# Moving a decoder step's merge gates ahead of the attention, and the sample's paged attention into the prompt's units

## The chip, the cores and the metric

One core of a Trainium2 chip runs the whole step as one program. The metric is device time in microseconds, as a median over runs. The engines are TensorE (PE; its weight loads are PEld), VectorE (DVE), ScalarE (ACT), GpSimd (POOL) and SyncE (SP, which here only issues transfers). A framework schedules the program ahead of time: each engine gets a fixed list of instructions, in an order that a scheduler chose from the order of the source, and runs it from top to bottom.

## What is computed

One layer of a hybrid decoder, for a prompt (1 sequence of 1024 tokens) and a sample (8 sequences of 4 new tokens, each with 8192 cached ones). Cut to what matters:

```python
h = rmsnorm(x, g_norm1) * (1 + scale1) + shift1          # scale, shift, gate: silu(c) @ w_ada
za, zq, zkv, zg, zm = split(h @ w_in)                    # u|v, q, k/v of 3 branches, branch gates, merge gates
ya = chunk_spatial_gating(u, layernorm(v))
kc, vc = compress_blocks(cached and new rows)            # one row per block of 64 tokens
o_cmp = softmax(q kc) vc                                 # its probabilities also choose 16 blocks
o_sel = softmax(q k_chosen) v_chosen                     # the sample: from the paged cache
o_win = softmax(q k_window) v_window                     # last 512 tokens
yb = g0 * o_cmp + g1 * o_sel + g2 * o_win
x = x + gate1 * ((sigmoid(zm_a) * (ya @ w_a) + sigmoid(zm_b) * (yb @ w_b)) @ w_out)
x = x + gate2 * conv_ffn(rmsnorm(x, g_norm2) * (1 + scale2) + shift2)
```

Shapes: d_model 1024, 8 query heads and 2 key heads of 64, 1056 columns (1024 prompt, 32 sample). All in float32; large products are made of three float32r products of high and low parts.

## The kernel before

Activations lie with features on partitions and the 1056 columns in the free dimension. A **dense output** is one 128-feature slice of h @ w_in: 8 k-tiles by 3 products by 3 column ranges (`CH`), 72 matmuls (`dense`, `products`). There are 22 of them behind u: four queries (`query`), two keys (`key`) and sixteen merge gates (`merge_gate`). Queries, keys and gates go to DRAM and are read back later.

A **compression step** `compress(n)`, n = 0 to 15, loads 32 pages of a sample sequence (4 MB, tensor `pcmp`, two such steps a sequence) into one of two buffers and runs 64 matmuls; `compress_end(n)` finishes it. Steps 9 to 15 stand in a loop over j = 0 to 6 (lines 719 to 728), each after two dense outputs. That loop holds all queries, both keys and gates 0 to 7. Then PG and R2B, the pools of the pages, are released.

Then comes the sample's attention (from line 737): the compressed branch with the choice of blocks, which gives the mask `MB`; two **windows** (`sample_window`, four sequences each, 2 MB); and 32 **paged pieces** (`sel_unit(b, u)`, four per sequence, each 16 pages or 2 MB of `psel`). A piece is a chain: scores (PE, line 869), mask and maximum (DVE, 870 and 872), exp (ACT, 873), four transposes (PE, 877), a copy out of PSUM (ACT, 878), 16 value matmuls (PE), a copy (ACT, 891). After u = 3 the four pieces are merged (897 to 921). The first eight pieces (`EARLY`) and gates 8 to 15 stand in the source one after the other; the scheduler interleaves them. Inside the gates stand three late modulation chunks (`ada_late`: 2 MB of `w_ada`, 8 matmuls of 512 columns and 4 small ones).

Last comes the prompt's attention: 32 **units** (i, j), query tile i = 0 to 7 of 128 rows and head pair j = 0 to 3. `attend_n(n)` makes scores, maxima, exponentials and scales of unit n; `combine_n(n - 2)` transposes (line 1113), copies (1116) and multiplies with the values for the unit two back. A unit of tile i works on i + 1 key tiles in the chosen branch and up to five in the window branch, so units grow from i = 0 to i = 7. `key_tiles(j)` reads a key back and splits it into high and low parts (lines 949 to 952); `queries(i)` does so for a query tile (966, 967). The remaining 24 pieces are put behind `combine_n`, six in each eight units, and five more modulation chunks at n = 1, 4, 12, 20 and 28. Pieces, windows and chunks share page-size buffers: two in pool R3S, and two more in R3C for half of the pieces once the gates are done.

Matmuls of the unit and of the piece are issued by the helper `mm`, which is line 55 for all of them. Pages are issued on SP (three of four groups for `psel`) and on ACT (`load_pages`).

Of the kernel before, what the change touches and what calls it, by code (L numbers as in the profile page):

```python
# [49 lines left out]
def step_kernel(tc, A):  # L50
# [30 lines left out]
    def slot(dt=F32):  # L81
        return S([128, R], dt, "S", NS)
# [146 lines left out]
    def ada_chunk(ch, tiles, per, own):  # L229
        ps = pU()  # L230
        for h in range(2):
            for g in range(4):
                k = 4 * h + g
                mm(ps[32 * g:32 * g + 32], sc[:, k], tiles[k // per][:, (k % per) * 512:(k % per + 1) * 512],
                   h == 0, h == 1)
        modev = own()
        act.copy(modev, ps)
# [4 lines left out]
        dve.tensor_tensor(mod[:, ch * 4:ch * 4 + 4], v[:, :, 0:9],  # L242
                          bada[:, ch * 4:ch * 4 + 4, None].to_broadcast([128, 4, 9]), op=OP.add)

# [449 lines left out]
    R2B = new_pool("r2b", "right")  # L694
# [24 lines left out]
    for j in range(7):  # L719
        if j < 4:  # L720
            query(j)
        elif j < 6:
            key(j - 4)
        else:
            merge_gate(7, slot())
        merge_gate(j, slot())
        compress(LATE + j)
        compress_end(LATE + j)
    PG.release()
    R2B.release()  # L730
# [3 lines left out]
    for b in range(8):  # L734
        pool.dma_start(A["o_wsv"][b][508:512], vs_new[4 * b:4 * b + 4, 128:256])


    R3 = new_pool("r3")
    R3S = new_pool("r3s")
    GR = C2([128, 2, 3])  # L740
# [3 lines left out]
    for gr in range(2):  # L744
# [16 lines left out]
        nm = R3([128, 1], F32, "sm1", 12)  # L761
        dve.tensor_reduce(nm, ps[:, 0:128], axis=AX.X, op=OP.max, negate=True)
        p = R3([128, 128], F32, "ou", 5)
        su = R3([128, 1], F32, "sm1", 12)
        act.activation(p, ps[:, 0:128], AF.Exp, bias=nm, accum_out=su)
        r = R3([128, 1], F32, "sm1", 12)
# [37 lines left out]
    def sample_window(gr):  # L804
        ps = pU()
        st = R3S([128, 4, 4, 256], F32, "st", 2).rearrange("p a b c -> p (a b c)")
        wk = st[:, 0:2048].rearrange("p (b n) -> p b n", b=4)
        wv = st[:, 2048:4096].rearrange("p (b k c) -> p b k c", b=4, c=128)
        act.dma_start(wk, A["wk"][4 * gr:4 * gr + 4].rearrange("b p n -> p b n"))
        for i in range(4):  # L810
            act.dma_start(wv[:, i], A["wv"][4 * gr + i].rearrange("(k p) c -> p k c", p=128))
# [10 lines left out]
        nm = R3([128, 1], F32, "sm1", 12)  # L822
        dve.tensor_reduce(nm, s, axis=AX.X, op=OP.max, negate=True)
        su = R3([128, 1], F32, "sm1", 12)
# [18 lines left out]
        dve.tensor_copy(ow, po[:, 0:128])  # L843
# [7 lines left out]
    def sel_unit(b, u):  # L851
        if u == 0:
# [3 lines left out]
        n = 4 * b + u  # L856
        st = R3C([128, 4, 4, 256], F32, "st", 2) if n in third else R3S([128, 4, 4, 256], F32, "st", 2)
        load_pages([(st[:, c, k], A["psel"], b * 64 + 16 * c + 4 * u + k) for c in range(4) for k in range(4)],
                   None, (3, 7))
        s = R3([128, 544], F32, "su", 2)  # L860
        n = 544 if u == 0 else 512
        if u == 0:
            pt = pU()
# [8 lines left out]
        dve.tensor_reduce(nm4[:, u:u + 1], s[:, 0:n], axis=AX.X, op=OP.max, negate=True)  # L872
        act.activation(s[:, 0:n], s[:, 0:n], AF.Exp, bias=nm4[:, u:u + 1], accum_out=s4[:, u:u + 1])  # L873
# [4 lines left out]
        act.copy(pst[:, 0:512], pt)  # L878
        if u == 0:
            pt = pU()  # L880
            pe.transpose(pt[0:32, 0:128], s[:, 512:544], ident)
            dve.tensor_copy(pst[0:32, 512:640], pt[0:32, 0:128])
        po = pU()
# [7 lines left out]
        act.copy(o, po[:, 0:128])  # L891
        outs.append(o)
        if u < 3:
            return

        nl = R3([128, 1], F32, "sm1", 12)
# [5 lines left out]
        nM = R3([128, 1], F32, "sm1", 12)  # L902
# [5 lines left out]
        su = R3([128, 1], F32, "sm1", 12)  # L908
# [3 lines left out]
        r = R3([128, 1], F32, "sm1", 12)  # L912
# [12 lines left out]
    def ada_late():  # L925
        ch = next(ada_next)
        st = R3S([128, 4, 4, 256], F32, "st", 2).rearrange("p a b c -> p (a b c)")
        for p0 in (0, 2048):
            sync.dma_start(st[:, p0:p0 + 2048], A["w_ada"][ch][:, p0:p0 + 2048])
        ada_chunk(ch, [st], 8, lambda: R3([128, 544], F32, "su", 2)[:, 0:512])  # L930

    third = set(n for n in range(EARLY, 32) if n % 4 in THIRD)
    sample_window(0)
    sample_window(1)
    for n in range(EARLY):
        sel_unit(n // 4, n % 4)
    KH, KL = [], []

    def key_tiles(j, anchor):
        k0, k1 = slot(F32R), slot(F32R)  # L940
        l0, l1 = slot(F32R), KX([128, NP], F32R) if j else slot(F32R)
        kr = slot()
        if anchor is not None:
            dve.tensor_copy(kr[0:1, 0:1], anchor[0:1, R - 1:R])
        sync.dma_start(kr[:, 0:NP], A["o_k"][j][:, 0:NP])
        f = kr[:, 0:NP]
        for h, k, l in ((0, k0, l0), (1, k1, l1)):
            own, other = slice(64 * h, 64 * h + 64), slice(64 - 64 * h, 128 - 64 * h)
            act.copy(k[own, 0:NP], f[own])
            dve.tensor_tensor(l[own, 0:NP], f[own], k[own, 0:NP].bitcast(F32), op=OP.subtract)  # L950
            dve.tensor_copy(k[other, 0:NP], k[own, 0:NP].bitcast(F32))
            dve.tensor_copy(l[other, 0:NP], l[own, 0:NP].bitcast(F32))
        KH.append((k0, k1))
        KL.append((l0, l1))

    def queries(i, l):

        c0 = 128 * i
        qs = slot(F32R)
        dve.tensor_copy(qs[0:1, 0:1], l[0:1, 0:1].bitcast(F32))  # L960
        for j in range(4):
            q = qt[j][:, c0:c0 + 128]
            for h in range(2):
                own, other = slice(64 * h, 64 * h + 64), slice(64 - 64 * h, 128 - 64 * h)
                c = (4 * h + j) * 128
                act.copy(qs[own, c:c + 128], q[own])  # L966
                dve.tensor_tensor(qs[other, c:c + 128], q[own], qs[own, c:c + 128].bitcast(F32), op=OP.subtract)
        return qs

    SGP = new_pool("sgp")  # L970
    for j in range(8, 16):
        if j == 13:
            key_tiles(0, None)
        if j == 14:
            q_first = queries(TILES[0], KL[0][0])
        sg = merge_gate(j, SGP([128, R], F32, "sg", 2))
        if j < 11:
            ada_late()
    SGP.release()
    W.release()  # L980
    KX = new_pool("kx", "right")
    R3C = new_pool("r3c", "right")


    key_tiles(1, sg)
    VV = [slot(), slot()]
    for i in range(2):
        dve.tensor_copy(VV[i][0:1, 0:1], sg[0:1, R - 1:R])
        sync.dma_start(VV[i][:, 0:1024].rearrange("p (k c) -> p k c", c=256),
                       A["o_rows"][1][512 * i:512 * i + 512].rearrange("(k p) c -> p k c", p=128))  # L990
# [147 lines left out]
    def sel_n(n):  # L1138
        if EARLY <= n < 32:
            sel_unit(n // 4, n % 4)  # L1140
# [19 lines left out]
    R3C.release()  # L1160
    KX.release()
    R3S.release()
# [13 lines left out]
    R3.release()  # L1176
# [312 lines left out]
```

## Time and profile before

| | us |
|---|---|
| median of 3 runs | 2117.55 |
| lowest, highest | 2116.81, 2118.93 |
| profiled execution | 2113.03 |
| its span | 2111.3 |
| PE busy in it | 1976.1 (94%) |
| DVE, ACT, POOL busy | 978.6, 760.9, 315.0 |

The span runs from the first to the last instruction; the rest of an execution's time lies around it. Stage by stage: the dense outputs begin at 304 us, the last compression step ends at 551, gate 15 ends at 676, the prompt's attention runs from there to 1153, and what follows (merge, output product, feed-forward) is dense.

Busy of PE is modelled: a matmul's end is drawn later than the next one's start, so a short wait can hide in it. The granted clock (PEclk) is a share of full speed: 0.5 is 1.2 GHz and 1.0 is 2.4 GHz. A span's mean lies between.

### The profile page before, as it was taken

How to read it: one execution, taken by the hardware profiler on the slowest of the kernel's cores; microseconds unless marked ns; L12 is line 12 of the kernel's file. 1: busy time of each engine (PE TensorE's matmuls, PEld its weight loads, DVE VectorE, ACT ScalarE, POOL GpSimd, SP SyncE). 2: the span in 40 equal slices, each digit the busy share in tenths (PEclk: the TensorE clock that was granted, in tenths of full speed). 3: DMA queues.
4: the chain of work that ended last, by engine and by line, in shares of the span. 5: the costliest groups of instructions: out<-in, count | busy, mean ns of one | idle time of the engine just before them, and what ended most of it. 6: DMA issues, size and time to landing. Idle time of an engine off the chain costs nothing.

```text
span 2111.3 us, 41204 instructions
## 1 busy us (share of the span) xinstructions
PE 1976.1 (94%) x15449; PEld 1810.8 (86%) x15449; DVE 978.6 (46%) x2246; ACT 760.9 (36%) x1628; POOL 315.0 (15%) x506
## 2 busy tenths in 40 slices
PE   5899898999998679799999999999999999999996
PEld 3899898999887446566668999999999999999996
DVE  6512420111233446567665668545354453453467
ACT  3311211111222336466764247542341432413433
POOL 3410010001000112133341310110010100100102
PEclk7899999999999589899999999999999999999998
DMA  8464568864636757636423633211121111111112
GB/s 306 138 205 158 169 218 257 265 221 142 197 109 204 252 212 235 211 120 206 142 84 121 230 105 131 73 65 60 51 80 42 49 46 45 51 46 45 36 53 83
DMA packets 217671, 288.35 MB, mean 137 GB/s; under 512 B 25504, under 2 KB 170048, under 8 KB 215296
## 3 DMA queue, kind: packets, MB, share of 16 engines
q1 hardware_dynamic: 149872, 203.69, 29.5%
q10 hardware_dynamic: 62320, 63.78, 9.6%
q0 software_dynamic: 5280, 18.26, 2.4%
q8 instruction: 122, 2.00, 0.4%
q14 instruction: 77, 0.63, 0.1%
HBM read 264.57 MB, written 25.21 MB: 137 GB/s over the span
## 4 chain that ended last, share of the span: by engine, by line
PE 81%; DMA 7%; DVE 5%; issue 3%; ACT 3%; ACTq 1%; SPq 0%; POOL 0%; DVEq 0%; POOLq 0%
PE t L55 77%; PE t L1113 3%; DMA t<-pcmp 2%; DMA t<-psel 1%; DMA t<-w_ada 1%; DMA t<-xT 1%; ACT t L1077 1%; PE t L877 1%; DVE t L306 1%; DVE t L1374 1%; ACTq L511 0%; ACT t L966 0%; DMA t<-o_k 0%; DVE t L1101 0%; DVE t L1076 0%
## 5 line engine op out<-in xcount | busy, mean ns | idle before, releaser
L55 PE MATMUL t<-t,t 128*128 128x384 f32 (+12 forms) x14738 | 1896.5, 321 | 90.9 <-DVE t L159 14.6
L55 PEld LDWEIGHTS t<-t,t 128*128 128x128 f32 (+2 forms) x14610 | 1729.7, 170 | 214.8 <-issue 104.7
L306 DVE TENSOR_TENSOR t<-t,t 128x512 fp32r<-128x512 f32 (+3 forms) x322 | 238.7, 748 | 382.2 <-ACT t L305 378.7
L305 ACT CAST t<-t 128x512 fp32r<-128x512 f32 (+3 forms) x322 | 205.0, 646 | 406.5 <-PE t L55 294.3
L1101 POOL TENSOR_SCALAR t<-t,t 128x384 f32<-128x384 f32 (+3 forms) x96 | 119.0, 1253 | 326.1 <-DVE t L1095 125.0
L1217 DVE SCALAR_TENSOR_TENSOR t<-t,t,t 128x384 f32<-128x384 f32 (+1 forms) x168 | 95.7, 571 | 109.8 <-PE t L55 109.4
L1076 DVE TENSOR_REDUCE t<-t 128x1 f32<-128x384 f32 (+3 forms) x192 | 95.9, 517 | 67.9 <-PE t L55 67.3
L1077 ACT ACTIVATE t<-t,t 128x384 f32<-128x384 f32 (+3 forms) x192 | 105.8, 559 | 34.3 <-DVE t L1076 18.3
L1286 ACT COPY t<-t 128x384 f32<-128x384 f32 x132 | 58.5, 443 | 142.6 <-PE t L55 142.6
L1116 ACT COPY t<-t 128x512 f32<-128x512 f32 (+1 forms) x136 | 77.5, 578 | 49.3 <-PE t L1113 35.4
L1295 POOL COPY t<-t 128x2 f32<-128x2 f32 x44 | 19.1, 433 | 435.4 <-ACT t L1286 435.4
L1300 DVE SCALAR_TENSOR_TENSOR t<-t,t,t 128x1072 f32<-128x1072 f32 x44 | 58.7, 1334 | 53.6 <-ACT t L1299 53.6
L1113 PE MATMUL t<-t,t 128*128 128x128 f32 x528 | 83.4, 283 | 0.1
L1113 PEld LDWEIGHTS t<-t,t 128*128 128x128 f32 x528 | 57.2, 141 | 17.7 <-issue 16.4
L1299 ACT ACTIVATE t<-t,t 128x1072 f32<-128x1072 f32 x44 | 56.5, 1284 | 28.6 <-DVE t L1288 27.7
L538 DVE TENSOR_SCALAR t<-t,t 128x64 f32<-128x64 f32 x16 | 4.5, 283 | 127.9 <-PE t L55 127.9
L1301 DVE SCALAR_TENSOR_TENSOR t<-t,t,t 128x1072 f32<-128x1072 f32 x44 | 58.7, 1333 | 1.4
L661 ACT ACTIVATE t<-t 128x384 f32<-128x384 f32 (+1 forms) x48 | 22.1, 463 | 95.0 <-PE t L55 84.2
L1101 DVE TENSOR_SCALAR t<-t,t 128x384 f32<-128x384 f32 (+3 forms) x96 | 50.0, 573 | 0.6
L533 ACT ACTIVATE t<-t,t 128x128 f32<-128x128 f32 x16 | 7.9, 494 | 110.1 <-PE t L55 99.0
L877 PE MATMUL t<-t,t 128*128 128x128 f32 x128 | 23.1, 310 | 23.1 <-ACT t L873 22.9
L873 ACT ACTIVATE t<-t,t 128x512 f32<-128x512 f32 (+1 forms) x32 | 23.4, 730 | 58.7 <-DVE t L872 30.5
(261 smaller groups left out, 949.1 us busy)
## 6 DMA issues: line engine op xcount, KB each, us to landing
t<-psel SPq DMA_DIRECT2D x384, 128.0 KB
t<-pcmp SPq DMA_DIRECT2D x320, 128.0 KB
t<-pcmp ACTq DMA_DIRECT2D x192, 128.0 KB
t<-w_up SPq DMA_DIRECT2D x88, 256.0 KB
t<-psel ACTq DMA_DIRECT2D x128, 128.0 KB
t<-w_ada SPq DMA_DIRECT2D x16, 1024.0 KB
t<-t SPq DMA_DIRECT2D x28, 528.0 KB
t<-w_t ACTq DMA_DIRECT2D x52, 256.0 KB
```

The costliest lines, as they stand in the source:

```text
L55: return pe.matmul(out, lhsT, rhs, start=start, stop=stop)
L305: act.copy(hi, t)
L306: dve.tensor_tensor(lo, t, hi.bitcast(F32), op=OP.subtract)
L1076: dve.tensor_reduce(nm, bk, axis=AX.X, op=OP.max, negate=True)
L1077: act.activation(P[:, w:w + n], bk, AF.Exp, bias=nm, accum_out=s8[:, branch, h, c:c + 1])
L1101: (dve if e == "d" else pool).tensor_scalar(P, P, fc, None, op0=OP.mult)
L1113: pe.transpose(pt[:, 256 * a + 128 * h:256 * a + 128 * h + 128], P[:, c:c + 128], ident)
L1116: act.copy(pp[:, 0:n], pt[:, 0:n])
L1217: dve.scalar_tensor_tensor(x[:, a:e], ps[:, 0:e - a], gate[:, f, 0:1], base[:, a:e], op0=OP.mult, op1=OP.add)
L1286: act.copy(up[:, 2 + a:2 + e], ps[:, 0:e - a])
L1300: dve.scalar_tensor_tensor(acc[:, 0:w], up[:, 1:1 + w], cw[:, n, 1:2], acc[:, 0:w], op0=OP.mult, op1=OP.add)
L1301: dve.scalar_tensor_tensor(acc[:, 0:w], up[:, 2:2 + w], cw[:, n, 2:3], acc[:, 0:w], op0=OP.mult, op1=OP.add)
```

## The change

All 22 dense outputs become a list `fill`, and four of it are taken ahead of each of the steps 9 to 13; the two that are left follow step 13. So no dense output is left for the sample's attention. Keys and queries are read back and split before steps 14 and 15, which have no dense work beside them in the source. The sample's compressed branch stays where it was in the source. Windows go to n = 0 and 1 of the prompt's units. Each piece is cut into `sel_scores`, `sel_turn` and `sel_values`: scores of piece m at n = m + 2, its transposes one n later ahead of that n's scores, and its values in the same n behind `combine_n`. All eight modulation chunks stand at n = 1, 5, ... 29. Windows, pieces and chunks take one of four buffers of R3S in turn (`page_buffer`), which lie where the pages of the compression lay; a piece's ACT transfers are held behind the last use of its buffer. The piece's copy out of PSUM goes from ACT to DVE, the window's last copy from DVE to ACT, and the windows' transfers from ACT's queue to SP's. R3, the pool of small tiles, moves to the side where the next stage's weights are put.

```diff
-    for j in range(7):
-        if j < 4:
-            query(j)
...
-        merge_gate(j, slot())
-        compress(LATE + j)
-        compress_end(LATE + j)
+    fill = [lambda j=j: query(j) for j in range(4)] + [lambda j=j: key(j) for j in range(2)]
+    fill += [lambda j=j: merge_gate(j, slot()) for j in range(16)]
+    fill = iter(fill)
+    R2B = new_pool("r2b")
+    for n in range(9, 14):
+        for _ in range(4):
+            next(fill)()
+        compress(n)
+        compress_end(n)
+    for f in fill:
+        f()
...
+    W.release()
+    KX = new_pool("kx", "right")
+    R3 = new_pool("r3", "right")
...
+    key_tiles(0, None)
+    key_tiles(1, None)
+    VV = [slot(), slot()]
...
+    q_first = queries(TILES[0], KL[0][0])
+    for n in (14, 15):
+        compress(n)
+        compress_end(n)
+    R2B.release()
+    PG.release()
...
+    def page_buffer():
+        n = len(uses)
+        uses.append(None)
+        return n, R3S([128, 4, 4, 256], F32, f"st{n % 4}", 1), uses[n - 4] if n >= 4 else None
...
-        act.dma_start(wk, A["wk"][4 * gr:4 * gr + 4].rearrange("b p n -> p b n"))
+        sync.dma_start(wk, A["wk"][4 * gr:4 * gr + 4].rearrange("b p n -> p b n"))
...
-        act.copy(pst[:, 0:512], pt)
-        if u == 0:
+        dve.tensor_copy(pst[:, 0:512], pt)
+        if n % 4 == 0:
...
-    sels = iter(range(EARLY, 32))
-    for n in range(len(units) + AHEAD):
+    held, turned = {}, {}
+
+    def sel_first(m):
+        if 0 < m <= 32:
+            turned[m - 1] = sel_turn(m - 1, held[m - 1][2])
+        if 0 <= m < 32:
+            held[m] = sel_scores(m)
+
+    def sel_second(m):
+        if 0 < m <= 32:
+            use, st, _ = held.pop(m - 1)
+            sel_values(m - 1, use, st, turned.pop(m - 1))
+            if m % 4 == 0:
+                sel_merge(m // 4 - 1)
+
+    for n in range(len(units) + AHEAD + 1):
         attend_n(n)
+        if n < 2:
+            sample_window(n)
+        sel_first(n - 2)
         combine_n(n - AHEAD)
-        if n % 8 in (0, 2, 3, 5, 6, 7):
-            sel_n(next(sels, 32))
-        if n in (1, 4, 12, 20, 28):
+        sel_second(n - 2)
+        if n % 4 == 1 and n < 32:
             ada_late()
```

**Where instructions stand now.** First TensorE at compression step 15 (`64x128`, 16 in a row; tile `t_6501` or `t_7318` is the page buffer, `t_563` to `t_566` the compression's weights). Before, dense outputs stand on both sides:

```order
L55 MATMUL t_6473<-t_588,t_6412 128x288
L55 MATMUL t_6606<-t_6501,t_563 64x128 x16
L55 MATMUL t_6606<-t_6501,t_564 64x128 x16
L55 MATMUL t_6606<-t_6501,t_565 64x128 x16
L55 MATMUL t_6606<-t_6501,t_566 64x128 x16
L55 MATMUL t_7766<-t_595,t_7762 128x384
```

In the change, TensorE from the last dense matmul on (`t_7138` is the buffer of step 14; `t_7667` the first unit's scores):

```order
L55 MATMUL t_7037<-t_588,t_6976 128x288
L55 MATMUL t_7243<-t_7138,t_563 64x128 x16
L55 MATMUL t_7243<-t_7138,t_564 64x128 x16
L55 MATMUL t_7243<-t_7138,t_565 64x128 x16
L55 MATMUL t_7243<-t_7138,t_566 64x128 x16
L55 MATMUL t_7513<-t_7511,t_84 128x4
L55 MATMUL t_7310<-t_7308,t_573 64x64 x2
L55 MATMUL t_7314<-t_573,t_7308 64x64 x2
L55 MATMUL t_7423<-t_7318,t_563 64x128 x16
L55 MATMUL t_7423<-t_7318,t_564 64x128 x16
L55 MATMUL t_7423<-t_7318,t_565 64x128 x16
L55 MATMUL t_7423<-t_7318,t_566 64x128 x16
```

Steps 14 and 15 now follow the last dense output directly, and the prompt's first unit follows step 15. Next TensorE at a paged piece, before (piece 4, of sequence 1: the new keys, scores `32x512`, transposes L877, the new keys' transpose L881, values `32x128`, and piece 5's scores):

```order
L55 MATMUL t_7416<-t_4106,t_4104 32x32 x4
L55 MATMUL t_7422<-t_7362,t_4104 32x512 x4
L877 MATMUL t_7431<-t_69,t_7415 128x128 x4
L881 MATMUL t_7437<-t_69,t_7415 32x128
L55 MATMUL t_7440<-t_7362,t_7430 32x128 x16
L55 MATMUL t_7440<-t_605,t_7430 32x128
L55 MATMUL t_7514<-t_7460,t_4104 32x512 x4
```

And in the change (piece 1's transposes L939, piece 2's scores `t_8281`, a query tile's transpose L1029, a unit's transposes L1122, piece 1's values `t_8303`):

```order
L55 MATMUL t_8679<-t_76,t_72 128x128
L939 MATMUL t_8221<-t_69,t_8101 128x128 x4
L55 MATMUL t_8281<-t_8227,t_4101 32x512 x4
L1029 MATMUL t_8180<-t_69,t_8167 128x128
L1122 MATMUL t_8291<-t_69,t_7884 128x128 x2
L1122 MATMUL t_8291<-t_69,t_7897 128x128 x2
L55 MATMUL t_8303<-t_8048,t_8220 32x128 x16
```

Other work now stands between a piece's steps. Last SP's queue at the end of the compression, before (`t_6501` step 15's pages, `t_4103` the stored queries, `o_k` the first key, then pieces):

```order
L511 DMA t_6501<-pcmp 128x256
L733 DMA t_6683<-t_4103 128x1056
L733 DMA t_6684<-t_4103 128x1056
L733 DMA t_6685<-t_4103 128x1056
L733 DMA t_6686<-t_4103 128x1056
L945 DMA t_8282<-o_k 128x1024
L501 TENSOR_LOAD t_560
L511 ISA
L511 DMA t_6972<-psel 128x256
```

And in the change:

```order
L772 DMA t_7083<-t_4100 128x1056
L744 DMA t_7092<-o_k 128x1024
L744 DMA t_7106<-o_k 128x1024
L777 DMA t_7116<-o_rows 128x4x256
L777 DMA t_7117<-o_rows 128x4x256
L867 DMA t_7701<-wk 128x4x512
L869 DMA t_7701<-wv 128x4x128 x4
L867 DMA t_7800<-wk 128x4x512
L869 DMA t_7800<-wv 128x4x128 x4
L997 DMA t_7862<-w_ada 128x2048 x2
```

Both keys, the values, both windows and a modulation chunk now stand ahead of the first piece on SP.

## Rows read from the trace of the kernel before

**Rows 1.** The page: busy by engine; 40 slices of granted clock and of traffic.

```profile
PE 1976.1 (94%) x15449; PEld 1810.8 (86%) x15449; DVE 978.6 (46%) x2246; ACT 760.9 (36%) x1628; POOL 315.0 (15%) x506
PEclk7899999999999589899999999999999999999998
GB/s 306 138 205 158 169 218 257 265 221 142 197 109 204 252 212 235 211 120 206 142 84 121 230 105 131 73 65 60 51 80 42 49 46 45 51 46 45 36 53 83
```

**Rows 2.** Windows by stage: start:end, length, each engine's busy and count, clock, DMA.

```profile
core 0: us, PE busy (x) PEld busy (x) DVE busy (x) ACT busy (x) POOL busy (x), PEclk, DMA share, GB/s
304.00:498.00 194.00, 185.82 (x1752) 181.12 (x1753) 25.87 (x53) 32.45 (x66) 8.75 (x14) 0.98 0.75 238
498.00:560.00 62.00, 62.00 (x566) 60.17 (x564) 9.48 (x20) 9.77 (x19) 6.34 (x12) 1.00 0.48 159
560.00:675.00 115.00, 110.83 (x881) 99.79 (x880) 36.43 (x93) 30.81 (x69) 3.73 (x7) 0.99 0.45 147
675.00:760.00 85.00, 52.62 (x406) 31.98 (x405) 35.44 (x108) 23.64 (x76) 7.28 (x11) 0.68 0.83 279
760.00:881.00 121.00, 101.49 (x961) 65.60 (x963) 73.14 (x219) 64.01 (x187) 29.94 (x22) 0.89 0.61 194
881.00:1100.00 219.00, 211.78 (x2142) 149.46 (x2143) 144.87 (x429) 150.80 (x441) 69.64 (x56) 1.00 0.48 149
1100.00:1153.00 53.00, 52.57 (x462) 44.78 (x460) 31.00 (x79) 27.31 (x55) 12.67 (x8) 1.00 0.39 132
```

**Rows 3.** PE's waits by releaser, 675 to 881: total, times, longest.

```profile
PE t L877 <- ACT t L873: 22.3, 9, 5.3
PE t L55 <- DVE t L918: 7.6, 3, 3.4
PE t L55 <- DMA t<-psel: 1.7, 2, 1.4
```

**Rows 4.** Windows inside the light half of the attention, as Rows 2.

```profile
700.00:740.00 40.00, 25.61 (x187) 17.48 (x186) 18.20 (x64) 15.14 (x57) 6.62 (x10) 0.59 0.84 270
740.00:760.00 20.00, 14.26 (x98) 6.55 (x98) 4.64 (x15) 1.76 (x3) 0.12 (x1) 0.76 0.88 339
800.00:840.00 40.00, 37.94 (x371) 26.25 (x371) 31.05 (x93) 25.82 (x74) 14.08 (x10) 1.00 0.78 234
880.00:920.00 40.00, 38.83 (x440) 29.12 (x436) 23.84 (x74) 26.70 (x79) 8.94 (x8) 1.00 0.79 249
```

**Rows 5.** Groups by form, one gate's stretch 372.8 to 384.2: busy, mean ns.

```profile
L55 PE MATMUL t<-t,t 128*128 128x384 f32 x48 | 8.6, 337 | 0.0
L55 PE MATMUL t<-t,t 128*128 128x288 f32 x25 | 3.6, 295 | 0.0
```

**Rows 6.** The same for one compression step, 384.5 to 391.3.

```profile
L55 PE MATMUL t<-t,t 128*64 128x128 f32 x128 | 7.2, 273 | 0.0
```

**Rows 7.** PE's waits by releaser, 300 to 675.

```profile
PE t L55 <- DMA t<-pcmp: 8.0, 1, 8.0
```

**Rows 8.** DVE groups by form, 560 to 1153: splits of keys and queries, the piece's mask.

```profile
L870 DVE TENSOR_TENSOR t<-t,t 128x512 f32<-128x512 f32 x32 | 22.0, 687 | 42.8 <-PE t L55 42.5
L967 DVE TENSOR_TENSOR t<-t,t 64x128 fp32r<-64x128 f32 x64 | 18.5, 292 | 3.7 <-ACT t L966 1.7
L950 DVE TENSOR_TENSOR t<-t,t 64x1024 fp32r<-64x1024 f32 x4 | 4.9, 1217 | 7.9 <-PE t L55 5.9 <-ACT t L949 2.0
L952 DVE CAST t<-t 64x1024 fp32r<-64x1024 f32 x4 | 2.7, 687 | 0.1
```

**Rows 9.** Groups by form, 1108 to 1153: the next stage's dense matmuls.

```profile
L55 PE MATMUL t<-t,t 128*128 128x384 f32 x96 | 19.3, 344 | 0.2 <-DVE t L306 0.2
L55 PE MATMUL t<-t,t 128*128 128x288 f32 x48 | 7.9, 299 | 0.0
```

**Rows 10.** ACT groups by form, 560 to 1153: the piece's copy out of PSUM.

```profile
L878 ACT COPY t<-t 128x512 f32<-128x512 f32 x32 | 19.0, 595 | 13.2 <-PE t L877 13.0
```

**Rows 11.** DVE's waits by releaser in the heavy half, 881 to 1100.

```profile
DVE t L1076 <- PE t L55: 47.8, 37, 5.5
```

More of the change, by code (lines that the diff above doesn't have):

```diff
@@ L236, in ada_chunk @@
         modev = own()
-        act.copy(modev, ps)
+        copied = act.copy(modev, ps)
         pt = pT()
@@ L717, in key, with key_tiles, queries @@
                 pool.dma_start(A["o_wsk"][b][:, 508:512], kr[:, NP + 4 * b:NP + 4 * b + 4])
[L719 to L730 removed]
+    fill = [lambda j=j: query(j) for j in range(4)] + [lambda j=j: key(j) for j in range(2)]
[9 more added lines that the diff above has]
+        f()
+    for b in range(8):
+        pool.dma_start(A["o_wsv"][b][508:512], vs_new[4 * b:4 * b + 4, 128:256])
+    W.release()
+    KX = new_pool("kx", "right")
+    R3 = new_pool("r3", "right")
+    KH, KL = [], []
+    def key_tiles(j, anchor):
+        k0, k1 = slot(F32R), slot(F32R)
+        l0, l1 = slot(F32R), KX([128, NP], F32R) if j else slot(F32R)
+        kr = slot()
+        if anchor is not None:
+            dve.tensor_copy(kr[0:1, 0:1], anchor[0:1, R - 1:R])
+        sync.dma_start(kr[:, 0:NP], A["o_k"][j][:, 0:NP])
+        f = kr[:, 0:NP]
+        for h, k, l in ((0, k0, l0), (1, k1, l1)):
+            own, other = slice(64 * h, 64 * h + 64), slice(64 - 64 * h, 128 - 64 * h)
+            act.copy(k[own, 0:NP], f[own])
+            dve.tensor_tensor(l[own, 0:NP], f[own], k[own, 0:NP].bitcast(F32), op=OP.subtract)
+            dve.tensor_copy(k[other, 0:NP], k[own, 0:NP].bitcast(F32))
+            dve.tensor_copy(l[other, 0:NP], l[own, 0:NP].bitcast(F32))
+        KH.append((k0, k1))
+        KL.append((l0, l1))
+    def queries(i, l):
+        c0 = 128 * i
+        qs = slot(F32R)
+        dve.tensor_copy(qs[0:1, 0:1], l[0:1, 0:1].bitcast(F32))
+        for j in range(4):
+            q = qt[j][:, c0:c0 + 128]
+            for h in range(2):
+                own, other = slice(64 * h, 64 * h + 64), slice(64 - 64 * h, 128 - 64 * h)
+                c = (4 * h + j) * 128
+                act.copy(qs[own, c:c + 128], q[own])
+                dve.tensor_tensor(qs[other, c:c + 128], q[own], qs[own, c:c + 128].bitcast(F32), op=OP.subtract)
+        return qs
     qt = [slot() for _ in range(4)]
@@ L842, in sample_window @@
         ow = R3([128, 128], F32, "ou", 5)
-        dve.tensor_copy(ow, po[:, 0:128])
+        uses[use] = act.copy(ow, po[:, 0:128])
         pt = pT()
@@ L890, in sel_unit, with sel_merge @@
         o = R3([128, 128], F32, "ou", 5)
[L891 to L896, printed above, removed]
+        uses[use] = act.copy(o, po[:, 0:128])
+        sel_state[b][2].append(o)
+    def sel_merge(b):
+        nm4, s4, outs = sel_state[b]
+        nl = R3([128, 1], F32, "sm1", 8)
         dve.tensor_reduce(nl, nm4, axis=AX.X, op=OP.min)
@@ L935, in step_kernel @@
[L935 to L990, printed above, removed]
+        uses[use] = ada_chunk(ch, [st], 8, lambda: R3([128, 544], F32, "su", 2)[:, 0:512])
```

65 lines of the change are left out of this document (33 added, 32 removed).

## The prediction

> **What bounds the kernel now.** I read the page first: TensorE is busy 1976 of 2111 us, so only what PE waits for, or runs slowly through, can be won [rows 1]. Its total work does not change: the change adds no matmul. Then the windows by stage [rows 2]. From 304 to 675 us PE is full except for one wait of 8.0 us for pages [rows 7]. From 881 to 1100 it is full too, at clock 1.00, and DVE there waits 47.8 us for PE [rows 11]: PE sets that pace, 2142 matmuls in 219 us, 0.102 us each. The loss sits between: from 675 to 881 PE runs 406 + 961 = 1367 matmuls in 206 us, 0.151 us each, 67 us more than at the later pace. Three things are mixed there. The paged pieces are serial chains, and PE waits 22.3 us for their exponentials alone [rows 3]. Eight pieces and four modulation chunks crowd in, the transfers run at 0.84 to 0.88 share [rows 4]. And the clock: mean grant 0.68 from 675 to 760, near the 1.2 GHz level, after PE was idle 32 of 85 us [rows 2].
>
> **The change part by part.** All sums are against the profiled execution, 2113.03 us, which lies 4.5 us under the median of the runs, 2117.55; I add that back at the end.
>
> *Dense outputs moved forward.* A gate is 48 matmuls of 384 and 24 of 288 columns in about 11.7 us (72 of the stretch's 73 rows in 11.4 us plus its edges) [rows 5], a compression step 128 matmul rows in 7.2 us [rows 6] and some 0.45 us of small ones. All 22 dense outputs with steps 7 to 13 take 22 x 11.7 + 7 x 7.65 = 311 us from 304, so 615. The 8.0 us page wait ahead of step 8 [rows 7] shrinks, since three dense outputs stand before that step and not two; I keep 3 us: the last gate ends at 618. Pages of steps 10 to 15 have four dense outputs (47 us) for 4 MB, so I cost them at nothing; uncovered they'd cost 14 us a step at 290 GB/s. Steps 14 and 15 run to 633.
>
> *Start-up of the attention.* Now something is late that was hidden behind gates. Queries, keys and values come back only when the slots of h are free, after the last gate: 4 x 528 KB and 2 x 512 KB at 270 to 339 GB/s [rows 4] are 9 to 12 us. Then DVE splits both keys, 4 subtractions of 1.22 us and 8 casts of 0.69 us, and the first queries, 8 of 0.29 us [rows 8]: 12.7 us, some beside the second key's transfer. So the first unit starts 22 to 25 us after the last gate, and PE idles 7 to 10 us after step 15. Then DVE sets the pace until the first piece: the choice of blocks for two groups, two windows, and five or six light units. From 560 to 675 DVE spent 36.4 us on windows, choice, three pieces and one key [rows 2]; I take the same 36 us for this mix plus little. So the first piece's scores run 62 us after the last gate, at 680; bounds 45 (windows landed, DVE dense) and 85 (one transfer or split chain more).
>
> *The rest of the attention.* From 675 to 1153 PE ran 406 + 961 + 2142 + 462 = 3971 rows [rows 2], of which 144 are the next stage's dense ones [rows 9]: 3827. Three pieces of some 48 rows ran before 675, so all units, pieces and chunks are about 3970. Some 80 of them run in the start-up. The other 3890 at 0.102 us are 397 us. Pieces are 40% of these and 31% of the window from which the pace comes, and a piece's rows go four abreast; small light units switch oftener. I let the two cancel. In units 5 to 8 transfers are slower than PE: a unit now takes 2.5 MB (a piece and a quarter of a chunk), 10.6 us at 234 to 249 GB/s [rows 4], against 90 rows or 9.2 us: 5 us. At the end no dense matmul stands between the last combines any more; their copies show, and the first weights wait for R3's tiles: 4 us. End: 680 + 397 + 9 = 1086. Now the same point is 1153 less two dense outputs of 11.7 us [rows 9], 1129.6. **Gain 44 us.** What follows is the same.
>
> *Copies moved between engines.* 32 copies of 512 columns leave ACT, 0.595 us each [rows 10], for DVE, which takes 0.687 us for the same size out of PSUM [rows 8]: 22 us on DVE, 0 on the path, since DVE waits 47.8 us for PE in the heavy half and is busy 145 of 219 us [rows 2, 11]. If that cover is gone, it costs up to 22 us. The Trainium skill speaks against this edit: "VectorE: DVE Perf Modes", section "Why PSUM operands drop a tier", says that a PSUM source holds a float32 copy at one element a cycle, so the move buys no faster copy; the two rows above agree. Windows' transfers on SP: a few issues, nothing.
>
> *Buffers.* A piece's load waits for the last reader of its buffer four uses before; at 1.25 uses a unit of 9 to 15 us that leaves about 20 us of slack for an 8 us load. I cost it at nothing; rival 3 is its price.
>
> **The rivals.** (1) *Paged traffic sets the light half's pace.* Units 0 to 15 need 2.5 MB each. Rows of 234 to 249 GB/s speak for 10.6 us a unit; by the code a unit with its piece has 78, 90, 102 and 114 matmul rows for tiles 0 to 3, which PE runs in 8.0, 9.2, 10.4 and 11.6 us; 4 x (2.6 + 1.4 + 0.2) = 17 us are lost: 2090. Against: 270 and 339 GB/s were seen [rows 4]. (2) *The start-up and DVE cost more*: 85 us and not 62, or the moved copies show: 23 us, 2096. For: six units, choice and windows all hang on DVE. (3) *Slower: the light half keeps the pace it has now.* Place: pieces 1 to 17. If each piece's scores stand on PE ahead of pages that have not landed, PE stops in order, units behind it too, and the clock falls as it did at 0.59 from 700 to 740 [rows 4]. 16 units of 96 rows, 1540, at 0.151 and not 0.102 us are 75 us: 2147. It is slower than now from a pace of about 0.131 on. Against: 371 rows ran in 40 us from 800 to 840 at clock 1.00 beside 234 GB/s [rows 4], and the pieces' steps have other work between them. The Trainium skill has this as a rule: "TensorE: Matmul & The Clock Gate", section "HAM oscillation — how this bites in real kernels", a kernel whose work per tile is shorter than its wait for data runs cold in every tile. By it the light half would be the 2147 us case; the 700 to 740 row agrees, the 800 to 840 row does not. (4) *More is won*: start-up at 45 us, the lighter mix at 385 and not 397 us, no transfer loss: 34 us more, 2038. That the change doesn't move the work is not a rival: the rows of order show the gates gone, and the pieces cut.
>
> **How the numbers follow.** Forecast: 2113.03 - 44 + 4.5 = 2073, chance 0.48, own range 2055 to 2084. Rival 1, 2090: 0.16. Rival 2, 2096: 0.13. Rival 4, 2038: 0.13. Rival 3, 2147: 0.10. The range 2038 to 2102 leaves out rival 3 and half of rival 4. What a measurement can tell from no change is about 0.2%, 4 us: faster is under 2113.3. The first four cases but a sliver of the second are faster: 0.87; within, 0.03; slower, 0.10.
>
> **What would show it.** In the profile after: the last dense matmul of 128 x 288 near 618; a PE gap of 7 to 10 us after step 15, ended by DVE's query split; the first piece near 680; the wait for the piece's exponentials gone from 22 us to a few; clock 1.00 from about 690 on; 0.102 us a row through the light half too; the next stage's dense matmuls from 1086. The forecast is wrong if PE's waits for psel exceed 10 us (rivals 1 and 3), if DVE stops waiting for PE in the heavy half (rival 2), or if the stage that follows gets slower.

## The result and the profile after

The changed kernel takes 2092.62 us (median of 4 runs, 2090.08 to 2097.68), the kernel before 2117.45 beside it: ratio 0.9885, 95% interval 0.9865 to 0.9905, a gain of some 24 us where 44 were forecast. That lies outside the forecast's own range, 2055 to 2084, and inside the whole one, 2038 to 2102. The profiled execution took 2091.29 us with a span of 2089.4, 21.7 us less than that of before. Measured again on another chip the ratio was 0.987 (0.9838 to 0.9902). Chips differ by a few us, so the runs below are compared by their ratio to the kernel before on their own chip; 0.001 is 2.1 us.

The page of the profile after, to be held against [rows 1]:

```profile
PE 1984.5 (95%) x15449; PEld 1813.2 (87%) x15449; DVE 992.5 (48%) x2273; ACT 748.0 (36%) x1598; POOL 314.6 (15%) x506
PEclk7999999999996899999999999999999999999998
```

PE's busy time is 8 us more than before, over a span 22 us shorter; the clock's dip, a slice of 5 and two of 8 in the attention, is now one of 6 and one of 8: it is smaller, but it stayed. The windows by stage show where (columns as in [rows 2]):

```profile
304.00:498.00 194.00, 194.00 (x1639) 190.51 (x1638) 29.43 (x56) 35.69 (x72) 14.04 (x24) 1.00 0.65 209
560.00:614.00 54.00, 54.00 (x424) 53.34 (x423) 6.97 (x13) 8.87 (x18) 2.13 (x4) 1.00 0.45 145
614.00:697.00 83.00, 65.48 (x607) 49.00 (x605) 40.57 (x140) 25.32 (x80) 7.49 (x11) 0.71 0.54 177
697.00:760.00 63.00, 59.55 (x603) 39.59 (x600) 46.12 (x138) 36.95 (x115) 15.01 (x13) 0.95 0.82 264
760.00:860.00 100.00, 96.43 (x1035) 63.41 (x1035) 63.13 (x175) 52.74 (x148) 24.76 (x18) 0.98 0.80 250
860.00:1079.00 219.00, 210.12 (x2053) 141.04 (x2046) 150.18 (x439) 133.98 (x391) 66.13 (x52) 0.98 0.57 177
1079.00:1133.00 54.00, 50.13 (x376) 43.94 (x376) 25.97 (x60) 20.87 (x35) 5.66 (x4) 0.97 0.35 120
```

Read them from the top. The dense stretch is full to the last gate, at 614. From 614 to 697 nothing stands beside the start of the attention: PE is busy 65 of 83 us at a mean grant of 0.71. From 697 on it is full, with the pieces in it: 603 + 1035 rows in 163 us, 0.0995 us each, where [rows 2] had 0.151. PE's waits from 697 to 1079, against [rows 3] (total, times, longest):

```profile
PE t L55 <- DVE t L985: 3.1, 3, 1.7
PE t L1029 <- DVE t L1027: 2.8, 2, 2.6
PE t L939 <- ACT t L932: 1.6, 3, 0.7
```

L939 waiting for L932 is a piece's transposes waiting for its exponentials: 1.6 us, where L877 waited 22.3. Last the start-up itself, PE in order of time, first 614 to 640, then 656 to 692 (start, length, line, stationary and moving shape, count, idle before it and its releaser). L889 and L892 are the windows' transposes; most rows behind them are their value products:

```profile
626.09 11.47 PE L55 MATMUL t<-t,t 128*64 128x128 f32 x145 [3.49 <-DVE t L539]
...
657.56 5.51 PE L55 MATMUL t<-t,t 128*128 128x32 f32 x30
...
668.36 1.12 PE L889 MATMUL t<-t,t 128*128 128x128 f32 x4 [2.04 <-DVE t L885]
669.27 0.42 PE L892 MATMUL t<-t,t 128*32 128x128 f32 x1
670.06 11.64 PE L55 MATMUL t<-t,t 128*128 128x128 f32 x60 [0.37 <-DVE t L893]
684.78 1.08 PE L889 MATMUL t<-t,t 128*128 128x128 f32 x4 [3.08 <-DVE t L885]
```

Between 657 and 668 PE does little but short rows; then sixty rows take 11.64 us, and a second such block follows at 685. A block is named after its first row. Taken by form, 40 of the 60 are the first window's value products and take 9.9 us (670 to 682):

```profile
L55 PE MATMUL t<-t,t 128*32 128x128 f32 x32 | 7.6, 420 | 0.0
L55 PE MATMUL t<-t,t 32*32 32x128 f32 x8 | 2.3, 382 | 0.0
```

Sixteen others are the second window's scores. The second window's 40 products take 8.7 us, so the two windows' products take 18.6. The first piece's new keys come at 697.6 and its paged scores at 699.6. The next stage's dense matmuls start at 1102.73.

### The profile page after: what moved, and what is told of

Read it like the earlier page. It is cut to its first block, busy times and chain, and to the rows that moved or that the text cites. A ratio compares the mean times of both kernels' runs of the same rounds, so it can differ in the third digit from the quotient of the medians.

```text
span 2089.4 us, 41176 instructions
## 1 busy us (share of the span) xinstructions
PE 1984.5 (95%) x15449; PEld 1813.2 (87%) x15449; DVE 992.5 (48%) x2273; ACT 748.0 (36%) x1598; POOL 314.6 (15%) x506
## 4 chain that ended last, share of the span: by engine, by line
PE 85%; DVE 7%; DMA 4%; ACT 2%; issue 1%; SPq 1%; ACTq 0%; DVEq 0%
PE t L55 81%; PE t L1122 3%; DMA t<-pcmp 2%; DVE t L1085 1%; PE t L939 1%; DMA t<-psel 1%; DVE t L1110 1%; SPq L512 1%; DVE t L1394 1%; DVE t L307 1%; DVE t L766 0%; DMA t<-xT 0%; DMA t<-w_bb 0%; ACT t L306 0%; DVE t L1253 0%
## 5 line engine op out<-in xcount | busy, mean ns | idle before, releaser
L307 DVE TENSOR_TENSOR t<-t,t 128x512 fp32r<-128x512 f32 (+5 forms) x322 | 240.8, 755 | 439.3 <-ACT t L306 436.2
L306 ACT CAST t<-t 128x512 fp32r<-128x512 f32 (+5 forms) x322 | 205.2, 646 | 421.2 <-PE t L55 311.4
L1122 PE MATMUL t<-t,t 128*128 128x128 f32 x528 | 90.2, 293 | 0.0
L1122 PEld LDWEIGHTS t<-t,t 128*128 128x128 f32 x528 | 59.7, 146 | 27.0 <-issue 22.6
L662 ACT ACTIVATE t<-t 128x384 f32<-128x384 f32 (+1 forms) x48 | 22.3, 465 | 133.1 <-PE t L55 98.4
L539 DVE TENSOR_SCALAR t<-t,t 128x64 f32<-128x64 f32 x16 | 4.5, 283 | 95.0 <-PE t L55 94.8
L1300 POOL MEMSET t<- 128x2 f32 x44 | 4.3, 99 | 253.7 <-DVE t L1321 156.1
L1225 POOL TENSOR_TENSOR t<-t,t 128x384 f32<-128x384 f32 (+1 forms) x24 | 28.0, 1173 | 83.2 <-DVE t L1224 81.1
```

Of the source, the lines that this page charges most:

```text
L306: act.copy(hi, t)
L307: dve.tensor_tensor(lo, t, hi.bitcast(F32), op=OP.subtract)
L1122: pe.transpose(pt[:, 256 * a + 128 * h:256 * a + 128 * h + 128], P[:, c:c + 128], ident)
```

## The experiments

Theory: taking the pieces apart wins the light half, as forecast, and the shortfall lies in the start-up, where the windows' rows were not costed. Rivals: paged traffic, the copies moved to VectorE, the tail, missing cover.

| run | what | ratio to before | 95% interval |
|---|---|---|---|
| a0_after | changed kernel again | 0.9870 | 0.9838 to 0.9902 |
| e5_whole | pieces not taken apart | 1.0042 | 1.0018 to 1.0066 |
| e3_once | pages of 30 pieces left out | 0.9836 | 0.9813 to 0.9859 |
| e4_turn | copy back on ScalarE | 0.9853 | 0.9830 to 0.9876 |
| e2_left | R3 on the left | 0.9900 | 0.9880 to 0.9920 |
| e11_nowin | windows left out | 0.9741 | 0.9714 to 0.9768 |
| e9_late | windows at turns 6, 7 | 0.9881 | 0.9852 to 0.9909 |
| e1_window, e15_window | windows' products reordered | 0.9801, 0.9811 | 0.9781 to 0.9821, 0.9790 to 0.9832 |
| e14_before_window | the same edit in the kernel before | 0.9947 | 0.9929 to 0.9966 |
| e7_cover | gates respread, one left as cover | 0.9879 | 0.9851 to 0.9906 |
| e12_cover2 | the same, transfers reordered | 0.9849 | 0.9823 to 0.9875 |

**Is the base the same?** The changed kernel was run again beside three of the others.

> The changed kernel itself, as the base of the other three on one chip (the earlier four ran on a chip whose kernel before took 2122.86 us, 5 us more than with the first measurement). All theories: 0.985 to 0.990 of the kernel before, first piece's scores at 697 to 700 us, next stage's dense matmuls from 1102 to 1106.

Ratio 0.9870; the first piece at 691.8 and the next dense stage at 1098.1, both some 5 us earlier than in the first profile and than expected, with 406 us between them for 405.

**Does the gain come from taking the pieces apart?**

```diff
-        sel_first(n - 2)
         combine_n(n - AHEAD)
-        sel_second(n - 2)
+        m = n - 2
+        if 0 <= m < 32:
+            use, st, s = sel_scores(m)
+            sel_values(m, use, st, sel_turn(m, s))
+            if m % 4 == 3:
+                sel_merge(m // 4)
```

> The changed kernel with the pieces not taken apart: scores, transposes, values and merge of a piece stand behind one another in one turn, as in the kernel before, everything else as changed. Theory F (the wait for the piece's exponentials, 22.3 us before and 1.6 us after, is what the taking apart wins): the wait comes back with 15 to 25 us and the whole is 12 to 25 us above the changed kernel. Rival G (the scheduler puts other work into the gap by itself, since no dense work crowds there any more): within 4 us of the changed kernel.

1.0042: slower than the kernel before, and 33 to 36 us above the changed one, more than the 12 to 25 of theory F. The taking apart is the whole gain and more; the rest of the change alone (dense outputs forward, everything else behind them) costs 9 us. Windows of this run, then PE's waits from 697 to 1079:

```profile
697.00:760.00 63.00, 48.86 (x510) 31.60 (x509) 40.64 (x116) 27.12 (x87) 13.21 (x12) 0.92 0.81 254
760.00:860.00 100.00, 87.70 (x873) 56.02 (x875) 60.28 (x165) 50.73 (x145) 21.10 (x15) 0.95 0.69 218
860.00:960.00 100.00, 89.20 (x840) 59.47 (x839) 59.63 (x183) 51.52 (x153) 23.25 (x20) 0.91 0.58 179
```

```profile
PE t L1029 <- DVE t L1027: 11.0, 6, 3.2
PE t L55 <- DVE t L985: 10.1, 5, 2.2
PE t L55 <- DVE t L976: 6.1, 4, 1.7
PE t L939 <- ACT t L932: 5.6, 4, 3.2
```

In 263 us PE runs 2223 rows where the changed kernel runs some 2580, is idle 37 us, and the grant sinks to 0.91 to 0.95. The wait that returns is only to a quarter the one named (L939, 5.6 us). The query tiles' softmax (L1027) and the merges (L976, L985) come late as well; that in whole pieces their small steps stand back to back in the lists fits this, but no run shows that it is the reason. So taking apart is worth more than was expected, and its place is wider than the exponentials.

**Does paged traffic set the pace (rival 1)?**

```diff
-        use, st, after = page_buffer()
-        load_pages([(st[:, c, k], A["psel"], b * 64 + 16 * c + 4 * u + k) for c in range(4) for k in range(4)],
-                   after, (3, 7))
+        if n < 2:
+            fixed.append(R3S([128, 4, 4, 256], F32))
+            load_pages([(fixed[n][:, c, k], A["psel"], b * 64 + 16 * c + 4 * u + k) for c in range(4) for k in range(4)],
+                       None, (3, 7))
+        use, st = n, fixed[n % 2]
```

> The changed kernel with the pages of pieces 2 to 31 left out (they use the pages of the first two pieces, so the selected branch of the sample's attention is computed on the wrong pages). Theory B (paged transfers contend): the heavy half, 0.1067 us a row where the prediction had 0.102, falls to 0.102 or less, and the light half too; 1,000 to 3,900 rows at 0.005 us give 10 to 20 us: 2072 to 2083 us. Theory C (the rows themselves cost this, whatever the transfers do): within 4 us of the changed kernel, 2088 to 2093 us.

0.9836 (two executions), 7 to 10 us under the changed kernel, with intervals that touch or overlap: between the two expectations. The windows tell the halves apart; the first two and the last two answer to the changed kernel's 603 and 1035 rows, and to its 944 and 933 rows at 199 and 166 GB/s in the same stretches:

```profile
697.00:760.00 63.00, 59.74 (x640) 38.90 (x640) 48.30 (x141) 37.49 (x116) 16.91 (x14) 0.97 0.22 87
760.00:860.00 100.00, 97.58 (x1056) 67.57 (x1055) 67.22 (x190) 58.42 (x168) 23.08 (x16) 1.00 0.17 65
860.00:960.00 100.00, 94.53 (x939) 61.52 (x937) 72.87 (x221) 58.33 (x178) 28.07 (x24) 0.98 0.11 39
960.00:1060.00 100.00, 95.37 (x914) 63.45 (x913) 64.55 (x170) 55.03 (x157) 32.52 (x24) 0.97 0.02 7
```

Without the traffic the light half runs 58 rows more in 163 us, some 6 us; the heavy half runs none more. Traffic is a small term of the light half and does not set the pace.

**Do the moved copies delay VectorE (rival 2)?**

```diff
-        dve.tensor_copy(pst[:, 0:512], pt)
+        act.copy(pst[:, 0:512], pt)
```

> The changed kernel with the copy behind the pieces' transposes put back from VectorE to ScalarE. Theory D (the moved copies delay VectorE's reductions in the heavy half): 2080 to 2089 us. Theory E (VectorE has room, ScalarE has not): 32 copies of about 595 ns come back to ScalarE, 19 us of its time, of which the part that a unit's exponentials wait for shows: 2092 to 2100 us.

0.9853 lies inside the interval of the changed kernel's second measurement and just below that of the first: between nothing and some 7 us in favour of ScalarE, not told apart. It excludes theory E's loss of several us, and nothing here makes these copies worth the 22 us of the bound. But the halves answer in opposite directions. The windows of this run, then of the changed kernel:

```profile
700.00:860.00 160.00, 149.41 (x1544) 97.57 (x1544) 98.36 (x290) 92.36 (x266) 38.92 (x30) 0.97 0.79 251
860.00:1079.00 219.00, 213.72 (x2100) 141.83 (x2101) 141.01 (x425) 143.36 (x412) 68.17 (x53) 1.00 0.55 173
```

```profile
700.00:860.00 160.00, 153.74 (x1614) 101.42 (x1608) 108.64 (x309) 89.10 (x261) 39.78 (x30) 0.97 0.80 254
860.00:1079.00 219.00, 210.12 (x2053) 141.04 (x2046) 150.18 (x439) 133.98 (x391) 66.13 (x52) 0.98 0.57 177
```

With the copy on ScalarE the heavy half runs 47 rows more, some 5 us, and the light half 70 fewer, some 7 us. The changed kernel run again and the two runs with reordered windows, all with the copy on VectorE, have 2044 to 2063 rows in the heavy stretch. So theory D holds for the heavy half, as far as one profile tells, and the light half takes the gain back.

**Is the tail lost to R3's place?** R3 is made on the left, behind the release of the compression's pages and under R3S, and released behind RY.

```diff
-    R3 = new_pool("r3", "right")
...
+    R3 = new_pool("r3")
     R3S = new_pool("r3s")
```

> The changed kernel with the working pool R3 put back on the left side, where the kernel before had it, so that the next stage's weights don't lie over tiles that the last combines still use. Theory T (the tail is lost to that placement): dense rows of w_ba run between the rows of the last two combines again, as they did before; from combine 7,2's first row to the end of the first dense group it took 62.0 us before and 68.1 us after, with another 2 us of wait behind it, so 6 to 8 us come back: 2084.5 to 2087 us. Rival: the weights' split or the transfers set the first dense row, not the placement: 2091 to 2094 us.

The mechanism came as expected. PE at the tail of this run, dense rows (128x384) among the last combines' transposes (L1122):

```profile
1095.37 1.12 PE L1122 MATMUL t<-t,t 128*128 128x128 f32 x4
1096.14 1.81 PE L55 MATMUL t<-t,t 128*128 128x384 f32 x13
1097.88 0.66 PE L1122 MATMUL t<-t,t 128*128 128x128 f32 x4
```

From combine 7,2's first row to the end of the first dense group it takes 62.8 us, and 68.1 in the changed kernel. But the whole is no faster, 0.9900: the first unit of the heavy half starts at 809.1 and not at 797 to 801, so the 5 us and more were lost before. Why the light half is slower with R3 there was not settled. The theory of the tail stands for the tail and wins nothing.

**What do the windows cost?** The two windows are left out here, with their transfers, so the sample's output lacks that branch.

```diff
     def sample_window(gr):
+        pt = pT()
+        mm(pt[:, 0:128], OC[gr], ident, True, True)
+        dve.tensor_copy(YCW[:, gr], pt[:, 0:128])
```

> The changed kernel with the two sample windows left out (their transfers, 130 matmul rows and the chains between; the window branch of the sample's attention is missing from the output). It prices the item that the prediction's start-up had as work of VectorE alone. Theory A2 (the windows cost the tensor engine what their rows and waits take, wherever they stand: 11.4 + 10.1 us of rows and 5.7 us of waits in the changed kernel run again): 24 to 30 us below the changed kernel, ratio 0.973 to 0.976 of the kernel before. Theory D2 (VectorE's chains set the start-up, as predicted, and the windows' rows are hidden in them): 5 to 12 us below, ratio 0.981 to 0.985.

0.9741: 27 to 30 us, as A2 expected and not D2. The last gate ends at 610.7, the first piece follows at 662.7, 52 us behind it and not 83. VectorE does not hide the windows' rows; PE pays for them. (This prices the windows whole, with their transfers and chains; the rows alone are changed below.)

**Is it their place, at a low clock and without cover?**

```diff
-        if n < 2:
-            sample_window(n)
+        if n in (6, 7):
+            sample_window(n - 6)
```

> The changed kernel with the two sample windows, their products in the old order, at turns 6 and 7 and not 0 and 1. Theory A1 (what the start-up loses is the low clock and the lack of cover there): the windows' 22.4 us of value products become about 11.5 us at full clock, the 6 us of waits around them vanish, and the whole is 12 to 18 us below the changed kernel. Theory A2 (it is the serial order of the products alone, wherever they stand): 0 to 5 us below.

0.9881, no gain: A2. The first piece now comes at 663.5, 50 us behind the last gate, close to the prediction's lower bound of 45, and it is worth nothing. The windows run from 688 to 735. Their value products take 13.8 us there for 18.6, so a part of what A1 counts on came, but the waits did not vanish: PE waits three times for 3.1 to 3.4 us between 692 and 725, and the grant is 0.90 and 0.88:

```profile
668.00:700.00 32.00, 28.29 (x288) 18.36 (x287) 24.65 (x73) 18.68 (x61) 7.44 (x8) 0.90 0.87 274
700.00:760.00 60.00, 52.43 (x469) 32.46 (x468) 30.28 (x81) 20.56 (x62) 8.66 (x7) 0.88 0.65 200
```

**Is it the order of their products?** All value products of one sample stood behind one another, in the same 32 output rows; now four samples alternate.

```diff
-        for i in range(4):
-            v = wv[:, i]
-            for k in range(4):
-                mm(po[32 * i:32 * i + 32, 0:128], pst[:, 128 * k + 32 * i:128 * k + 32 * i + 32], v[:, k], k == 0, False)
-            mm(po[32 * i:32 * i + 32, 0:128], pst[0:32, 512 + 32 * i:544 + 32 * i], vs_new[:, 128:256], False, True)
+        for k in range(4):
+            for i in range(4):
+                mm(po[32 * i:32 * i + 32, 0:128], pst[:, 128 * k + 32 * i:128 * k + 32 * i + 32], wv[:, i, k], k == 0, False)
+        for i in range(4):
+            mm(po[32 * i:32 * i + 32, 0:128], pst[0:32, 512 + 32 * i:544 + 32 * i], vs_new[:, 128:256], False, True)
```

> The changed kernel with one edit: the value products of the two sample windows run chunk by chunk with the four samples inside (four blocks of 32 output rows abreast), not sample by sample. Theory A (the start-up is set by the tensor engine's own uncovered work at a low granted clock): the two runs of 47 rows that took 11.87 and 10.58 us at 668 and 685 fall to about 3 us each (the pieces' values, written in this order, take 1.08 us for 32 rows), the first piece's scores come at about 683 instead of 699.6, and the whole goes from 2092.6 to 2074 to 2079 us. Theory B (paged transfers set the pace of the pieces): the first piece comes earlier but the pieces wait for pages instead, and the whole stays at 2088 to 2092 us.

> The changed kernel with the same edit, a second measurement on the chip of the run beside it: 0.978 to 0.983 of the kernel before if the first (0.9801) stands; the edit's own worth in the changed kernel is then the distance to 0.987 to 0.9885, 10 to 17 us.

0.9801 and 0.9811, 12 to 18 us under the changed kernel, as theory A had it; at 2080 to 2081 us this beats both kernels. The first piece came at 688.4 and not at 683. The same 60 rows that took 11.64 us:

```profile
669.96 1.12 PE L889 MATMUL t<-t,t 128*128 128x128 f32 x4 [1.85 <-DVE t L885]
670.87 0.42 PE L892 MATMUL t<-t,t 128*32 128x128 f32 x1
671.66 5.64 PE L55 MATMUL t<-t,t 128*128 128x128 f32 x60 [0.37 <-DVE t L893]
680.33 1.09 PE L889 MATMUL t<-t,t 128*128 128x128 f32 x4 [3.03 <-DVE t L885]
```

They take 5.64 us, and the waits ahead of them (L889, 1.85 and 3.03 us) stay. By form, the 40 value products fall from 9.9 to 2.6 us:

```profile
L55 PE MATMUL t<-t,t 128*32 128x128 f32 x32 | 1.9, 421 | 0.0
L55 PE MATMUL t<-t,t 32*32 32x128 f32 x8 | 0.7, 417 | 0.0
```

Both windows together fall from 18.6 to 5.2, and these 13.4 us are about what the whole gains. The Trainium skill has the rule ("TensorE: Matmul & The Clock Gate", section "Why this matters for your kernels": small-M matmuls whose outputs lie in distinct blocks of 32 partitions run side by side). These rows agree and add a condition: with the same outputs and operands, they gain only where neighbours in the list differ in their block.

In the kernel before, where the windows stand beside dense work at full clock:

> The kernel before with the one edit to the windows' value products (chunk by chunk, four samples inside). There the two windows stand beside dense work at full clock, 7.4 us of rows each. Theory A2 (the order of these products costs the tensor engine wherever it is full): 47 rows fall from about 5.8 to 2.2 us, 7 us for both, ratio 0.9965 (0.995 to 0.998). Theory A3 (what the edit wins in the changed kernel is won only because nothing covers the windows there): ratio 0.999 to 1.001.

0.9947, 11 us (7 to 15): A2 again, and more than the 7 us expected. By form, the 40 products of a window take 5.8 us in the kernel before and 1.5 here, 8.6 us for both. Serial products cost PE there too; a covered chain still uses PE's time where PE is the bound.

**Would cover help?** In the next two runs three dense outputs stand before each compression step, so that one gate is left behind step 15; the choice of blocks and the windows (reordered) are called ahead of it, R3 and two page buffers lie on the left, and the other two buffers, the keys and the values follow the last gate.

```diff
-    for n in range(9, 14):
-        for _ in range(4):
+    for n in range(9, 16):
+        for _ in range(3):
             next(fill)()
         compress(n)
         compress_end(n)
...
+    sample_window(0)
+    sample_window(1)
     for f in fill:
         f()
```

> Three dense outputs of h, not four, before each of the compression steps 9 to 15, so that one gate is left behind step 15; the choice of blocks and both windows (value products chunk by chunk, samples inside) are called ahead of that gate, R3 lies on the left, and two of the four page buffers come only when the dense weights are gone. Theory A (the start-up is lost because nothing covers its serial chains): 83 us from the last gate to the first piece fall to 45 to 55, and the whole is 20 to 30 us below the changed kernel, 2063 to 2073 of its 2092.6. Rival H (the pages of steps 10 to 15 no longer land in time with three outputs a step): PE waits for pcmp by 5 to 15 us come at steps 10 to 15 and eat half of it: 2076 to 2085.

0.9879. The waits of PE from 631 to 690, then of ACT from 615:

```profile
PE t L55 <- ACT t L830: 12.6, 1, 12.6
PE t L55 <- DVE t L761: 10.0, 1, 10.0
```

```profile
ACT t L830 <- DMA t<-psel: 16.1, 1, 16.1
```

ACT's copy inside the choice of blocks was late, and what it is charged with waiting for is a page transfer that ACT itself issues ahead of it. The first unit came at 683. With the first four pieces' pages on SP alone, behind keys and values:

```diff
-                   after, (3, 7))
+                   after, (3, 7) if n > 3 else (), VV_in[-1] if n < 4 else None)
```

> The run with one gate kept behind step 15 again, with one edit: the first four pieces' pages go to SP's queue alone and behind the loads of keys and values, so that no page transfer stands on ScalarE ahead of the copy in the choice of blocks (that copy waited 16.1 us for psel there) and the second key's load, issued at 660, does not stand behind twelve page transfers. Theory Q (the cover was there, and the queues' order lost it): the first unit starts at 645 to 655 and not 683, the whole comes to 2065 to 2078 us. Rival R (the work of the start-up is the tensor engine's own rows, so cover has little to give): 2083 to 2090 us.

0.9849, and 0.9801 to 0.9811 had the reordered windows without cover: this arrangement does not help, though its first piece comes at 679.5, 49 us behind the last gate, inside the 45 to 55 of theory A. It does not price cover alone: R3 lies on the left here, and with that edit alone the heavy half began 8 to 12 us later. The queue was part of it (first unit at 664.6; some 6 us won, the intervals overlap), but another wait took its place; PE's waits, and the windows behind the last gate, which ended at 631:

```profile
PE t L871 <- DVE t L867: 11.2, 1, 11.2
```

```profile
631.00:665.00 34.00, 14.38 (x181) 8.24 (x182) 21.90 (x60) 9.28 (x21) 0.53 (x1) 0.65 0.95 330
665.00:697.00 32.00, 29.82 (x296) 21.87 (x295) 24.01 (x89) 17.44 (x66) 5.05 (x8) 0.84 0.65 190
```

The window's transposes (L871) now wait for VectorE's scaling (L867). The gate is over before the choice is, and PE is idle 20 of 34 us. No page wait came at steps 10 to 15, so rival H falls.

## Why the prediction was right, and short by 20 us

*The bound and the mechanism: right.* The loss sat in the light half, between 675 and 881 [rows 2]; there the pieces' chains starved PE, and taking them apart removes that. e5 shows it: without that edit nothing is left. The named wait fell from 22.3 [rows 3] to 1.6 us. But in e5 only a quarter of it returns, so the exponentials that the prediction names are one part of what whole pieces cost.

*Dense stretch: right.* Last gate 614.3 for 618; the page wait of [rows 7] went altogether, not by 5 of 8 us. Step 15 ended at 636 for 633: PE waited 3.5 us ahead of it for VectorE's end of step 14 (L539), and step 15 took 10 us, not 7.2 [rows 6], at a lower grant (0.84 from 614 to 636). The first unit started 22 us after the last gate, as forecast; but by another path. The gap of 7 to 10 us behind step 15 did not come: PE ran on into the unit without a wait, so the later end of step 15 set its start, and not VectorE's splits.

*Start-up: the step that failed.* 62 us were forecast from the last gate to the first piece, as 25 plus VectorE's 36, and 83.3 came. VectorE's work was no more than thought: busy 40.6 us from 614 to 697, the splits included, for which the sum has 12.7 beside the 36. But it did not set the pace. PE was busy 65.5 of these 83 us, at 0.71 of its clock. The windows' 130 matmul rows stood in no term: in [rows 2] they lay among the dense rows of 560 to 675, and the sum took "all units, pieces and chunks" without them. e11 prices the windows at 27 to 30 us, and without them the start-up is 52 us; e1 gets 12 to 18 us back by the order of their products alone. e9 shows that the milestone itself is worth nothing: what counts is PE's total, and the rows come back wherever they stand.

*The rest, 406 us: right in sum, by luck.* From 697.6 to 1102.7 it took 405, for 3873 rows where the sum has 3890. The parts missed in both directions and cancelled: the light half ran at 0.0995 us a row and not 0.102 plus 5 us for transfers, the heavy one at 0.1067 (2053 rows in 219 us; before 0.102, 2142 rows [rows 2]). The 5 us for transfers are near e3's 6. Transfers do not account for the heavy half's pace (e3). The copies on VectorE account for about half of it: with them on ScalarE the same stretch runs at 0.1043 and at a grant of 1.00 (e4, one profile). The cause of the other half stays open; whether the larger share of pieces plays a part, which the sum let cancel against the small units, was not tested.

*Clock: half right.* 0.95 from 697 and 0.98 later, not 1.00 from 690.

*Tail and after.* The next dense stage starts at 1102.7; before, by the same reckoning, 1129.6: 27 us, of which 21.7 remain at the end. The prediction had the following stage unchanged. PE waits 2.2 us for the weights' copy just ahead of that first row and 2.1 us later for another split, by PE's waits from 1100 to 1205:

```profile
PE t L55 <- ACT t L306: 2.2, 1, 2.2
PE t L55 <- DVE t L1224: 2.1, 1, 2.1
```

In the sum: 1086 forecast, plus 21 for the start-up, less 4 for the earlier gate, less 1, gives 1102.7; the other 5 us were lost behind it, 2.1 of them in the second wait. Seen whole, from the first transpose of unit (7, 2) to the last instruction the same 6122 rows took 997.0 us before (from 1114.4) and take 1006.7 now (from 1082.7): the end costs some 10 us where the sum has 4.

*Rivals.* Rival 1's time (2090) was closest and its mechanism is not the cause (e3: 6 us of its 17). Rival 2's first half is what happened: a start-up of 85 us; but it blamed VectorE, and the cause is PE's own rows. Rival 3's pace of 0.151 did not come: the row of [rows 4] from 800 to 840 was the right one to trust. The copies cost nothing that shows in the whole time; VectorE's reductions still wait for PE in the heavy half, but for 25.8 us and not the 47.8 of [rows 11], and there the copies do show (e4).

## What to carry to other kernels

When work is moved away from beside a full engine, add its own rows on that engine to the sum: cover hides a wait, but not the time of the engine that is the bound. An earlier milestone is no gain if the work it passed comes later on the same engine. Small matmuls with 32 output rows should be written so that neighbours in the list fall into different blocks, first of all where they stand alone.

## What was not expected of the hardware

The 40 value products of a window took 9.9 us in one order and 2.6 in the other, with the same operands. From 668 to 697 PE was busy 24.8 of 29 us, and the grant still was 0.62, near the 1.2 GHz level; from 636 to 668 it had been busy 22.5 of 32 us, at 0.70. Within the 60 rows, from 670.06 to 681.70, PE has no idle time at all, at 0.58. The serial order is not needed for it: reordered, the same 60 rows ran at 0.54. In e9, with the windows at 688 to 735, the grant of 700 to 760 is 0.88, where the changed kernel had 0.94; whether the products or the waits of 3 us beside them draw it down was not told apart. The changed kernel's start-up, end of it:

```profile
668.00:697.00 29.00, 24.81 (x128) 14.63 (x128) 3.27 (x10) 2.54 (x6) 0.00 (x0) 0.62 0.27 80
```

And no cost shows of the 166 to 199 GB/s of transfers beside the heavy half: at 7 to 39 GB/s PE ran no more rows.
